# Four mixed layers on one core: weights staged further ahead, output tiles finished in pairs, elementwise work moved from GpSimd to VectorE

## The chip, the core and the metric

The kernel runs on one core of a Trainium2 chip. The core has five engines: TensorE for matrix products (PE in the profile; its weight loads are PEld), VectorE (DVE), ScalarE (ACT), GpSimd (POOL) and SyncE (SP), which here issues every DMA. The metric is the device time of one launch in microseconds. Three runs of the kernel before gave 3770.92 us in the median (3770.17 to 3778.2).

## What is computed

A sequence of 2048 tokens of width 1024, in float32, goes through four layers. Each has a wide input projection, several mixers, gates, an output projection and (but for the last) a layer norm over the residual sum. Cut to the frame, with the mixers left out:

```python
def first_block(x, w_in, lb_logits, hg_norm_w, sinks, w_out, ln_g, ln_b):   # layer 1
    h = jnp.einsum('btd,de->bte', h_res, w_in[layer])
    hq, hf, hi, hg, aq, ak, av, ag = jnp.split(h, IN_SPLITS, axis=-1)
    ...   # a gated linear recurrence (o_h) and a sliding-window attention (o_a)
    mix = jnp.concatenate([o_h, o_a], axis=-1)
    out = jnp.einsum('bte,ed->btd', mix, w_out[layer])
    z = DN_ALPHA * h_res.astype(f32) + out.astype(f32)
    mu = jnp.mean(z, axis=-1, keepdims=True)
    var = jnp.mean(jnp.square(z - mu), axis=-1, keepdims=True)
    z = (z - mu) * lax.rsqrt(var + LN_EPS)
    h_res = (z * ln_g[layer].astype(f32) + ln_b[layer].astype(f32)).astype(dt)

def reference(x, ...):
    x = first_block(x, ...)     # layer 1
    x = second_block(x, ...)    # layers 2 and 3: linear attention + spatial gating; retention + pooling
    return third_block(x, ...)  # layer 4: band attention, mLSTM, convolution; x + projection, no norm after
```

## The kernel before

**Blocks.** The tokens are cut into four blocks of 512. The blocks go in pairs: blocks 0 and 1 pass through layers 1, 2, 3 and 4 (layer 1 block 0, layer 1 block 1, layer 2 block 0, and so on), then blocks 2 and 3 do the same. So there are 16 block passes, eight per pair. Each pass loads its input (channels on the partitions, lines 521 to 549), runs the input projections, the mixers and the output projection (lines 575 to 648), and writes its result to DRAM twice: as channels (`chn`, the next layer's input) and as token rows (`rows`, the next layer's residual).

**Split numbers.** A product of float32 numbers is made of three matmuls on numbers of a shorter format: an operand is split in a high part and the rest, and high times high, high times rest and rest times high are added up in PSUM (line 324 issues each of them). For the input that is `ah` and `al`: ScalarE casts (line 548), VectorE subtracts (line 315, called by line 549).

**Weights.** A weight tile `whl` holds both parts of one piece of a weight matrix, 1 MB; there are four buffers of it. `weight` (line 439) is called for every piece. The first time that a piece is used, which is in block 0 of each layer, it is loaded unsplit into a staging tile `wst` (line 449; there are two of them), ScalarE casts it into the high half of `whl` (line 450), VectorE subtracts to get the other half (line 451, recorded as line 315), and the split pair is saved to DRAM as `wdr` (line 454). Every later use loads the split pair in one DMA, `whl<-wdr` (line 446). A `whl` buffer comes free when the last matmul that reads it is done, and only then can its next load start.

**Order of the work.** The program is written in straight Python; a scheduler in the framework places each instruction on its engine's queue by readiness and priority, and each engine then works its queue strictly in order. `weight` has a raised priority (`hp`, line 259), so weights are placed well ahead of their use. All DMAs are on SP's queue, in order too: a DMA that must wait for an engine holds up those behind it. In the first pass `load_x` keeps its DMAs in program order (lines 528 to 540): two quarter pieces of the input, a weight, two more pieces, a weight, and so on.

**The start of a pass.** Layer 1 to 4 all begin with `in_b4` (line 477): four weights give four groups of output channels, first for tokens 0 to 255 of the block (24 matmuls per group), then for tokens 256 to 511. Between the groups `flush` runs the pending pieces of the pass before (`tail`, line 650): a tail transposes one finished tile of 128 tokens on TensorE, copies it out on ScalarE, writes `chn`, applies the norm's scale and shift (lines 674 and 675, GpSimd, for tiles 0 and 2), and writes `rows`.

**The end of a pass.** The second half of the output projection (lines 609 to 643) takes four weights with two channel chunks each. It goes tile by tile: for each of the four tiles of 128 tokens all eight chunks, 24 matmuls, then on VectorE the residual sum (line 623), the norm's statistics (line 628), a chain of operations on one column (`rstd1`, line 702), and the normalisation (ScalarE for tiles 0 and 2, four VectorE operations for tiles 1 and 3). So every one of the four weights is in use until tile 3.

**GpSimd** has 408 elementwise operations with two inputs: the gates' products into `mix` (line 788 and the like), the rest parts of `split_ch` (line 570), scales and shifts, products of the rotary terms, sums of the pooling.

Of the kernel before, what the change touches and what calls it, by code (L numbers as in the profile page):

```python
# [10 lines left out]
F32 = mybir.dt.float32  # L11
# [215 lines left out]
class Build:  # L227
    def __init__(self, ctx, tc, I, O, layers=(1, 2, 3, 4), nblk=NB):
# [13 lines left out]
        self.parts = {}  # L242
# [196 lines left out]
    def weight(self, name, i, n=1024):  # L439
        nc = self.nc  # L440
        with self.hp():
            w = self.whl.tile([128, 2, n], F32R, tag="whl", name="whl")
            hi, lo = w[:, 0], w[:, 1]
            kept = self.parts.get((name, i))
# [3 lines left out]
            st = self.wst.tile([128, n], F32, tag="wst", name="wst")  # L448
            self.first(nc.sync.dma_start(st, self.I[name][i][:, 0:n]))
            nc.scalar.copy(hi, st)  # L450
            self.tt(lo, st, hi.bitcast(F32), ALU.subtract)
            if self.nblk > 1:
                kept = self.wdr.tile([128, 2, n], F32, tag=f"{name}_{i}", name="wdr")
                nc.sync.dma_start(kept, w.bitcast(F32))
                self.parts[name, i] = kept
        return hi, lo

# [63 lines left out]
    def load_x(self, b, l):  # L521
# [13 lines left out]
        self.ahead, self.start = ws, False  # L535

# [29 lines left out]
    def split_ch(self, p, k):  # L566
# [3 lines left out]
        self.tt(self.al[:, p], m, self.ah[:, p].bitcast(F32), ALU.subtract, self.nc.gpsimd)  # L570
# [4 lines left out]
    def out_proj(self, layer, b, split):  # L575
# [74 lines left out]
    def tail(self, layer, b, xr, t, lng, lnb):  # L650
# [132 lines left out]
    def gate_mix(self, accs, c0, n=512, half=None):  # L783
        for t in range(4):
# [3 lines left out]
            self.tt(m, m, g, ALU.mult, self.nc.gpsimd)  # L788
# [19 lines left out]
    def layer1(self, b, lc):  # L808
# [69 lines left out]
        for c in range(4):  # L878
# [3 lines left out]
            self.tt(m, m, g, ALU.mult, nc.gpsimd)  # L882
# [201 lines left out]
    def layer2(self, b, lc):  # L1084
# [86 lines left out]
        for t in range(4):  # L1171
# [5 lines left out]
            self.tt(s, s, sg, ALU.mult, nc.gpsimd)  # L1177
            self.tt(s, s, sb, ALU.add, nc.gpsimd)
        for t, ps in enumerate(self.in_a()):
            g = self.g()  # L1180
            self.gate(ps, g)
            self.tt(us[t], us[t], g, ALU.mult, nc.gpsimd)
# [78 lines left out]
    def layer3(self, b, lc):  # L1261
# [7 lines left out]
        for i in range(4):  # L1269
# [7 lines left out]
            self.tt(sh, sh, S, ALU.mult, nc.gpsimd)  # L1277
            self.tt(s, s, sh, ALU.add, nc.gpsimd)
# [8 lines left out]
        for g in range(4):  # L1287
# [9 lines left out]
            for l in range(g + 1):  # L1297
# [3 lines left out]
                self.tt(cur[:, start:528], prev[:, start:528], prev[:, start - d:528 - d], ALU.add, nc.gpsimd if l == 0 else None)  # L1301
# [497 lines left out]
```

## Time and profile before

| | |
|---|---|
| median of three runs | 3770.92 us (3770.17 to 3778.2) |
| the profiled execution | 3774.09 us |
| its span, first to last instruction | 3772.3 us |
| mean granted TensorE clock | 0.995 |
| TensorE busy | 3677.3 us, 20576 matmuls |
| VectorE busy | 2177.9 us, 5387 instructions |
| ScalarE busy | 1384.2 us, 2889 instructions |
| GpSimd busy | 542.1 us, 445 instructions |
| moved by DMA | 798.04 MB, 212 GB/s in the mean |

Busy times are sums over an engine's instructions; engines overlap. TensorE's busy time leaves 95 us of the span in which it has no matmul running. A row of a timeline gives the start, the duration, the engine, the line, the operation and its operands (out<-in), and in brackets how long the engine had been idle before it and what it waited for. A row with x2 or more stands for several instructions in a row, from the first one's start to the last one's end.

### The profile page before, as it was taken

The numbers are of one execution on the slowest core, as the hardware profiler recorded it, in microseconds if no ns is written. First come the engines' busy times: TensorE is split into PE (matmuls) and PEld (weight loads), VectorE is DVE, ScalarE is ACT, GpSimd is POOL, SyncE is SP. The second block draws the span as 40 slices with busy tenths as digits, with TensorE's granted clock in tenths as the row PEclk, the third lists the DMA queues.
The fourth block names the chain that finished last, engine by engine and source line by source line (L and its number), as shares of the span: only waits on it lengthen the run. The fifth ranks groups of instructions, "written<-read, shape, count | busy, mean of one in ns | idle before, by whom it ended". The sixth has DMA issues, their size and how long they took to land.

```text
span 3772.3 us, 53592 instructions
## 1 busy us (share of the span) xinstructions
PE 3677.3 (97%) x20576; PEld 3100.4 (82%) x20576; DVE 2177.9 (58%) x5387; ACT 1384.2 (37%) x2889; POOL 542.1 (14%) x445
## 2 busy tenths in 40 slices
PE   7999999999999999999999999999999999999999
PEld 6788888887888888788888878888887878888887
DVE  6765556555655598577456455443544545872873
ACT  5636343323241354325254263312221313441441
POOL 0020111112121200300200201111121311011002
PEclk9999999999999999999999999999999999999999
DMA  6775567855886576752544645747565756435434
GB/s 229 261 263 177 187 239 273 311 199 195 300 304 215 213 260 223 261 197 101 208 179 164 226 152 187 255 161 256 185 231 206 253 193 246 146 140 209 177 123 157
DMA packets 161680, 798.04 MB, mean 212 GB/s; under 512 B 17936, under 2 KB 18064, under 8 KB 93840
## 3 DMA queue, kind: packets, MB, share of 16 engines
q1 hardware_dynamic: 161424, 794.62, 58.4%
q8 instruction: 162, 2.65, 0.3%
q14 instruction: 94, 0.77, 0.1%
HBM read 593.02 MB, written 201.52 MB: 211 GB/s over the span
## 4 chain that ended last, share of the span: by engine, by line
PE 49%; DVE 6%; DMA 2%; ACT 2%; issue 1%; POOL 0%; SPq 0%; DVEq 0%; POOLq 0%; ACTq 0%
PE acc L324 41%; PE mm L324 6%; PE mm L327 3%; DVE u L312 2%; DMA whl<-wdr 1%; DVE t L315 1%; ACT t L301 0%; DVE big L312 0%; DMA wst<-in_wo_dram 0%; DVE t L1034 0%; DVE ss L1400 0%; ACT u L301 0%; POOL mix L315 0%; DVE mix L312 0%; ACT u L1424 0%
## 5 line engine op out<-in xcount | busy, mean ns | idle before, releaser
L324 PE MATMUL acc<-whl,ah 128*128 128x512 f32 (+3 forms) x6144 | 1816.2, 380 | 15.1 <-DVE whl L315 4.1
L324 PEld LDWEIGHTS acc<-whl,ah 128*128 128x128 f32 x6144 | 1112.0, 188 | 242.9 <-issue 7.1
L324 PE MATMUL acc<-whl,al 128*128 128x512 f32 (+3 forms) x3072 | 1156.8, 377 | 0.0
L324 PE MATMUL acc<-ah,whl 128*128 128x256 f32 (+1 forms) x4096 | 1076.8, 346 | 46.0 <-DVE whl L315 17.3
L324 PEld LDWEIGHTS acc<-ah,whl 128*128 128x128 f32 x4096 | 707.1, 191 | 135.0 <-DVE whl L315 18.6
L324 PE MATMUL acc<-al,whl 128*128 128x512 f32 (+1 forms) x2048 | 699.2, 342 | 0.5 <-DVE al L315 0.2
L324 PEld LDWEIGHTS acc<-whl,al 128*128 128x128 f32 x3072 | 578.0, 188 | 114.0
L324 PEld LDWEIGHTS acc<-al,whl 128*128 128x128 f32 x2048 | 391.5, 191 | 40.5 <-issue 2.9
L315 DVE TENSOR_TENSOR whl<-wst,whl 128x1024 fp32r<-128x1024 f32 (+2 forms) x140 | 173.3, 1244 | 142.0 <-ACT whl L450 131.5
L315 POOL TENSOR_TENSOR big<-big,u 128x512 f32<-128x512 f32 x96 | 139.1, 1471 | 562.0 <-PE mm L327 421.6
L450 ACT CAST whl<-wst 128x1024 fp32r<-128x1024 f32 (+2 forms) x140 | 143.3, 1027 | 149.3 <-DMA wst<-in_wi_dram 76.1
L548 ACT CAST ah<-u 128x512 fp32r<-128x512 f32 x128 | 79.3, 619 | 307.0 <-PE acc L324 200.1
L312 DVE SCALAR_TENSOR_TENSOR g<-g,acc 128x512 f32<-128x512 f32 x80 | 54.6, 686 | 204.3 <-ACT g L301 204.2
L312 DVE SCALAR_TENSOR_TENSOR u<-mix,hdw,u 128x512 f32<-128x512 f32 x240 | 165.6, 742 | 0.1
L315 POOL TENSOR_TENSOR mix<-mix,g 128x512 f32<-128x512 f32 x56 | 77.4, 1385 | 592.2 <-DVE g L312 574.2
L312 DVE SCALAR_TENSOR_TENSOR big<-big,acc 128x512 f32<-128x512 f32 x128 | 86.7, 684 | 120.2 <-PE acc L324 118.5
L301 ACT ACTIVATE g<-acc 128x512 f32<-128x512 f32 x72 | 42.6, 596 | 232.0 <-PE acc L324 226.4
L301 ACT ACTIVATE t<-mm,cols 128x128 f32<-128x128 f32 (+2 forms) x272 | 99.6, 463 | 66.6 <-PE mm L327 62.7
L315 POOL TENSOR_TENSOR u<-u,lc 128x512 f32<-128x512 f32 (+1 forms) x64 | 68.0, 1070 | 326.1 <-issue 170.0
L315 DVE TENSOR_TENSOR al<-u,ah 128x512 fp32r<-128x512 f32 x128 | 89.7, 702 | 42.1 <-ACT ah L548 41.0
L324 PE MATMUL mm<-big,u 128*128 128x256 f32 (+2 forms) x616 | 94.3, 289 | 7.3 <-ACT big L923 1.8
L324 PEld LDWEIGHTS mm<-big,u 128*128 128x128 f32 x616 | 84.3, 191 | 16.0 <-ACT u L1424 3.2
(342 smaller groups left out, 4376.8 us busy)
## 6 DMA issues: line engine op xcount, KB each, us to landing
whl<-wdr SPq DMA_DIRECT2D x396, 1024.0 KB, 4.8
wdr<-whl SPq DMA_DIRECT2D x132, 1024.0 KB, 5.3
wst<-in_wi_dram SPq DMA_DIRECT2D x100, 512.0 KB, 6.9
rows<-big SPq DMA_DIRECT2D x48, 512.0 KB, 4.0
chn<-t SPq DMA_DIRECT2D x96, 256.0 KB, 6.3
u<-chn SPq DMA_DIRECT2D x96, 256.0 KB, 6.6
big<-rows SPq DMA_DIRECT2D x48, 512.0 KB, 7.1
wst<-in_wo_dram SPq DMA_DIRECT2D x32, 512.0 KB, 6.0
```

Of the source, the lines that this page charges most:

```text
L301: return self.nc.scalar.activation(out, in_, f, bias=bias, scale=scale)
L312: return self.nc.vector.scalar_tensor_tensor(out, in0, s, in1, op0, op1)
L315: return (eng or self.nc.vector).tensor_tensor(out, a, b, op)
L324: return self.nc.tensor.matmul(out, lhsT, rhs, start=start, stop=stop)
L327: return self.nc.tensor.transpose(out, in_, self.ident)
L450: nc.scalar.copy(hi, st)
L548: nc.scalar.copy(h, c4(st))
```

## The change

Three things are done, and they are independent of each other in the code.

First, the weights. `pieces` lists every piece in the order of use. When `weight` is called for a piece that is already kept in DRAM, it now looks at the next two pieces of the list; those that are used for the first time are staged at once (`stage` issues the load into `wst`), and their own call later finds them there. In the first pass the very first weight is loaded, cast and subtracted in two column halves, the saves to `wdr` are held back (`unsaved`) and issued after the input is loaded with a lowered priority, and the layer's constants `lc` are loaded after the input and the four weights.

Second, the output projection. In its second half the tiles go in pairs: tiles 0 and 1 share one pass over the eight chunks, then tiles 2 and 3.

Third, all 408 elementwise operations of GpSimd go to VectorE. GpSimd keeps the setup, masks, fills and one small copy.

```diff
@@ -239,7 +239,7 @@
         self.bp = pool("bp", 1)
         self.dp = pool("dp", 1, space=bass.MemoryType.DRAM)
         self.wdr = pool("wdr", 1, space=bass.MemoryType.DRAM)
-        self.parts = {}
+        self.parts, self.staged, self.unsaved = {}, {}, []
         self.ps_a = pool("ps_a", 4, space=PSUM)
         self.ps_m = pool("ps_m", 4, space=PSUM)
 
@@ -441,19 +441,55 @@
         with self.hp():
             w = self.whl.tile([128, 2, n], F32R, tag="whl", name="whl")
             hi, lo = w[:, 0], w[:, 1]
+
+            assert self.order.pop(0) == (name, i, n)
+            if not self.start:
+                for a, k, m in self.order[0:2]:
+                    if (a, k) not in self.parts and (a, k) not in self.staged and (name, i) in self.parts:
+                        self.staged[a, k] = self.stage(a, k, m)
             kept = self.parts.get((name, i))
             if kept is not None:
                 nc.sync.dma_start(w.bitcast(F32), kept)
                 return hi, lo
-            st = self.wst.tile([128, n], F32, tag="wst", name="wst")
-            self.first(nc.sync.dma_start(st, self.I[name][i][:, 0:n]))
-            nc.scalar.copy(hi, st)
-            self.tt(lo, st, hi.bitcast(F32), ALU.subtract)
+            st = self.staged.pop((name, i), None) or self.stage(name, i, n)
+            parts = 2 if self.start and i == 0 else 1
+            for p in range(parts):
+                c = slice(p * n // parts, (p + 1) * n // parts)
+                nc.scalar.copy(hi[:, c], st[:, c])
+                self.tt(lo[:, c], st[:, c], hi[:, c].bitcast(F32), ALU.subtract)
             if self.nblk > 1:
                 kept = self.wdr.tile([128, 2, n], F32, tag=f"{name}_{i}", name="wdr")
-                nc.sync.dma_start(kept, w.bitcast(F32))
                 self.parts[name, i] = kept
+                self.unsaved.append((kept, w))
+                if not self.start:
+                    self.save()
         return hi, lo
+
+    def stage(self, name, i, n):
+        st = self.wst.tile([128, n], F32, tag="wst", name="wst")
+        parts = 2 if self.start and i == 0 else 1
+        for p in range(parts):
+            c = slice(p * n // parts, (p + 1) * n // parts)
+            self.first(self.nc.sync.dma_start(st[:, c], self.I[name][i][:, c]))
+        return st
+
+    def save(self):
+        while self.unsaved:
+            kept, w = self.unsaved.pop(0)
+            self.nc.sync.dma_start(kept, w.bitcast(F32))
+
+    def pieces(self):
+
+        for l, c in list(self.todo):
+            i = 0
+            for mode, cols in plan(l):
+                n = len(cols)
+                per = chunks_per_tile(n)
+                for _ in range(8 // per):
+                    yield f"wi{l}", i, per * n
+                    i += 1
+            for i in range(8):
+                yield f"wo{l}", i, 1024
 
     def next_w(self, n=1024):
         if self.ahead:
@@ -533,6 +569,9 @@
                     self.load_x1(b, l, t, i)
             ws.append(self.next_w())
         self.ahead, self.start = ws, False
+        self.lc = self.lconst(l, b)
+        with self.later(300):
+            self.save()
 
     def first(self, ins):
         if self.start:
@@ -567,7 +606,7 @@
 
         m = self.mix[:, (k - 4) * 1024 + 512:(k - 4) * 1024 + 1024]
         self.nc.scalar.copy(self.ah[:, p], m)
-        self.tt(self.al[:, p], m, self.ah[:, p].bitcast(F32), ALU.subtract, self.nc.gpsimd)
+        self.tt(self.al[:, p], m, self.ah[:, p].bitcast(F32), ALU.subtract)
 
     def mixv(self, t, k):
         return self.mix[:, t * 1024 + k * 128:t * 1024 + k * 128 + 128]
@@ -611,14 +650,13 @@
         for j in range(4):
             hi, lo = self.weight(wo, 4 + j)
             ws.append((hi.rearrange("p (k c) -> p k c", k=2), lo.rearrange("p (k c) -> p k c", k=2)))
-            if j == 0:
-                for i in range(2):
-                    for t in range(0):
-                        self.out_mm(acc[t], t, i, ws[0][0][:, i], ws[0][1][:, i])
-        for t in range(4):
-            for k in range(2 if t < 0 else 0, 8):
-                hi, lo = ws[k // 2]
-                self.out_mm(acc[t], t, k, hi[:, k % 2], lo[:, k % 2])
+        for t in range(4):
+
+            if t % 2 == 0:
+                for k in range(8):
+                    hi, lo = ws[k // 2]
+                    for t1 in (t, t + 1):
+                        self.out_mm(acc[t1], t1, k, hi[:, k % 2], lo[:, k % 2])
             x = self.xr[:, t, 512:1024]
             self.stt(x, x, alpha, acc[t], ALU.mult, ALU.add)
             if layer == 4:
@@ -671,8 +709,8 @@
         if t % 2 == 0:
             for i in range(2):
                 xi = x[:, i * 512:i * 512 + 512]
-                self.tt(xi, xi, lng[i], ALU.mult, nc.gpsimd)
-                self.tt(xi, xi, lnb[i], ALU.add, nc.gpsimd)
+                self.tt(xi, xi, lng[i], ALU.mult)
+                self.tt(xi, xi, lnb[i], ALU.add)
         nc.sync.dma_start(self.rows[layer, b % 2][t], x)
 
     def rms_row(self, b, xr):
@@ -785,7 +823,7 @@
             g = self.g((128, n)) if t < 2 else self.u((128, n))
             self.gate(accs[t][:, 0:n], g, 0.5 if half is None else half[:, t:t + 1])
             m = self.mix[:, t * 1024 + c0:t * 1024 + c0 + n]
-            self.tt(m, m, g, ALU.mult, self.nc.gpsimd)
+            self.tt(m, m, g, ALU.mult)
 
     def v_from(self, accs, scale=None):
         with self.hp():
...
@@ -1467,7 +1505,7 @@
...
-            self.tt(m, m, halves(g), ALU.mult, nc.gpsimd)
+            self.tt(m, m, halves(g), ALU.mult)
@@ -1487,8 +1525,8 @@
...
-            self.tt(x, x, cg_, ALU.mult, nc.gpsimd)
-            self.tt(x, x, cb_, ALU.add, nc.gpsimd)
+            self.tt(x, x, cg_, ALU.mult)
+            self.tt(x, x, cb_, ALU.add)
...
@@ -1750,13 +1788,14 @@
...
         self.todo = [(l, c) for b in range(0, self.nblk, 2) for l in self.layers for c in range(b, b + 2)]
         self.lc = None
+        self.order = list(self.pieces())
```

Three places show how this moves instructions. The first is SP's queue at the very start: `u` are pieces of the input, `wst` the unsplit weights, `lc` the constants, `wdr` the saved split weights. Before:

```order
L346 DMA cols_89<-in_cols_dram 128x293
L545 DMA u_193<-in_xt_dram 128x512
L545 DMA u_197<-in_xt_dram 128x512
L449 DMA wst_202<-in_wi1_dram 128x1024
L730 DMA lc_253<-in_lc1_dram 128x1280
L454 DMA wdr_206<-whl_201 128x2048
L545 DMA u_208<-in_xt_dram 128x512
L545 DMA u_212<-in_xt_dram 128x512
L449 DMA wst_217<-in_wi1_dram 128x1024
L454 DMA wdr_221<-whl_216 128x2048
L545 DMA u_223<-in_xt_dram 128x512
```

And after the change:

```order
L346 DMA cols_89<-in_cols_dram 128x293
L584 DMA u_193<-in_xt_dram 128x512
L584 DMA u_197<-in_xt_dram 128x512
L473 DMA wst_202<-in_wi1_dram 128x512 x2
L584 DMA u_210<-in_xt_dram 128x512
L584 DMA u_214<-in_xt_dram 128x512
L473 DMA wst_219<-in_wi1_dram 128x1024
L584 DMA u_224<-in_xt_dram 128x512
L584 DMA u_228<-in_xt_dram 128x512
L473 DMA wst_233<-in_wi1_dram 128x1024
L584 DMA u_238<-in_xt_dram 128x512
```

The saves and the constants no longer stand among the input's pieces, and the first weight comes in two halves.

The second is VectorE's queue where layer 1 of block 1 ends and layer 2 of block 0 begins. `acc` are output-projection sums, `big` is the residual tile, the one-column names (`vt`, `vy`, `vh`, `vf`, `mv`, `nm`) belong to the norm, `u_4378` to `u_4384` are its scales and shifts, and the `whl` that are made from `wst` are the next layer's first weights; the last two of the four that `in_b4` needs are shown. Before, at the end of tile 3:

```order
L312 SCALAR_TENSOR_TENSOR vt_4716<-vy_4715,vh_4713 128x1
L312 SCALAR_TENSOR_TENSOR vy_4715<-vt_4716,vy_4715 128x1
L312 SCALAR_TENSOR_TENSOR vt_4716<-vy_4715,vf_4714 128x1
L312 SCALAR_TENSOR_TENSOR vt_4716<-vt_4716 128x1
L312 SCALAR_TENSOR_TENSOR vy_4715<-vt_4716,vy_4715 128x1
L312 SCALAR_TENSOR_TENSOR big_3817<-big_3817,vy_4715,u_4380 128x512
L312 SCALAR_TENSOR_TENSOR big_3817<-big_3817,vy_4715,u_4381 128x512
L315 TENSOR_TENSOR whl_4872<-wst_4873,whl_4872 128x1024
L315 TENSOR_TENSOR whl_4931<-wst_4932,whl_4931 128x1024
```

After the change, from the residual sum of tile 3 (`acc_4542`); the subtraction of the third weight, `whl_4875`, stands two rows ahead of this piece, right behind tile 2's sum:

```order
L312 SCALAR_TENSOR_TENSOR big_3820<-big_3820,acc_4542 128x512
L321 TENSOR_SCALAR ve_4698<-mv_4696 128x1
L315 TENSOR_TENSOR al_97<-u_4757,ah_96 128x4x128
L321 TENSOR_SCALAR vy_4701<-ve_4698 128x1
L320 TENSOR_SCALAR vh_4699<-ve_4698 128x1
L320 TENSOR_SCALAR vf_4700<-ve_4698 128x1
L666 BN_STATS bst_4535<-big_3820 128x6
L312 SCALAR_TENSOR_TENSOR vt_4702<-vy_4701,vh_4699 128x1
L315 TENSOR_TENSOR al_97<-u_4765,ah_96 128x4x128
L312 SCALAR_TENSOR_TENSOR vy_4701<-vt_4702,vy_4701 128x1
L315 TENSOR_TENSOR big_3820<-big_3820,u_4381 128x512
L315 TENSOR_TENSOR whl_4934<-wst_4935,whl_4934 128x1024
```

The third and fourth weight stood behind tile 3's whole chain; now one stands ahead of tile 2's column chain, the other in the midst of it and ahead of tile 3's, and a scale of tile 0 (`u_4381`, an operation of GpSimd before) stands just ahead of the fourth.

The third is SP's queue at the same place: `whl<-wdr` is a kept weight, `wdr<-whl` a save, `wst` a weight to come, `chn` and `rows` the finished tiles. Before:

```order
L446 DMA whl_4546<-wdr_2292 128x2048
L676 DMA rows_123<-big_3817 128x1024
L454 DMA wdr_4769<-whl_4764 128x2048
L454 DMA wdr_4828<-whl_4823 128x2048
L449 DMA wst_4873<-in_wi2_dram 128x1024
L449 DMA wst_4932<-in_wi2_dram 128x1024
L670 DMA chn_122<-t_4800 128x512
L670 DMA chn_122<-t_4811 128x512
L676 DMA rows_123<-big_3817 128x1024
```

After the change:

```order
L452 DMA whl_4551<-wdr_2295 128x2048
L479 DMA wdr_4774<-whl_4771 128x2048
L473 DMA wst_4876<-in_wi2_dram 128x1024
L479 DMA wdr_4831<-whl_4828 128x2048
L473 DMA wst_4935<-in_wi2_dram 128x1024
L479 DMA wdr_4880<-whl_4875 128x2048
L473 DMA wst_5092<-in_wi2_dram 128x544
L708 DMA chn_122<-t_4805 128x512
L479 DMA wdr_4939<-whl_4934 128x2048
L473 DMA wst_5123<-in_wi2_dram 128x544
L708 DMA chn_122<-t_4816 128x512
L714 DMA rows_123<-big_3820 128x1024
```

The loads of the third and fourth weight stood behind two saves and behind a `rows` write; now each stands behind one save, and the `rows` write comes after the next layer's first loads.

More of the change, by code (lines that the diff above doesn't have):

```diff
@@ L881, in layer1 @@
             m = self.mix[:, c * 1024 + 512:c * 1024 + 1024]
-            self.tt(m, m, g, ALU.mult, nc.gpsimd)
+            self.tt(m, m, g, ALU.mult)
             for h in (c - 1, c, c + 1):
@@ L1176, in layer2 @@
                 self.ts(gs, gs, mv[:, 2 * i:2 * i + 1], y[:, i:i + 1], ALU.subtract, ALU.mult)
-            self.tt(s, s, sg, ALU.mult, nc.gpsimd)
-            self.tt(s, s, sb, ALU.add, nc.gpsimd)
+            self.tt(s, s, sg, ALU.mult)
+            self.tt(s, s, sb, ALU.add)
         for t, ps in enumerate(self.in_a()):
@@ L1181, in layer2 @@
             self.gate(ps, g)
-            self.tt(us[t], us[t], g, ALU.mult, nc.gpsimd)
+            self.tt(us[t], us[t], g, ALU.mult)
         for t in range(4):
@@ L1276, in layer3 @@
             self.tt(s, s, C, ALU.mult)
-            self.tt(sh, sh, S, ALU.mult, nc.gpsimd)
-            self.tt(s, s, sh, ALU.add, nc.gpsimd)
+            self.tt(sh, sh, S, ALU.mult)
+            self.tt(s, s, sh, ALU.add)
             self.tt(c4(s), c4(s), gt[:, i // 2, i % 2].unsqueeze(1).to_broadcast([128, 4, 128]), ALU.mult)
@@ L1300, in layer3 @@
                 cur = self.tb()
-                self.tt(cur[:, start:528], prev[:, start:528], prev[:, start - d:528 - d], ALU.add, nc.gpsimd if l == 0 else None)
+                self.tt(cur[:, start:528], prev[:, start:528], prev[:, start - d:528 - d], ALU.add)
                 prev = cur
@@ L1361, in layer4 @@
                 self.stt(ub[i][:, 32:544], th, 1.0, ca[i], ALU.add, ALU.mult)
-            self.tt(ub[i][:, 32:544], ub[i][:, 32:544], RS, ALU.mult, nc.gpsimd)
+            self.tt(ub[i][:, 32:544], ub[i][:, 32:544], RS, ALU.mult)
             nc.vector.tensor_copy(ub[i][:, 0:32], self.ch[:, i])
@@ L1506, in layer4 @@
             self.stt(m, ths[t], 1.0, m, ALU.add, ALU.mult)
-            self.tt(ths[t], m, m, ALU.mult, nc.gpsimd)
+            self.tt(ths[t], m, m, ALU.mult)
             nc.vector.tensor_reduce(ss[:, 4 * t:4 * t + 4].unsqueeze(2), c4(ths[t]), axis=AX.X, op=ALU.add)
@@ L1514, in layer4 @@
             m = self.mix[:, t * 1024 + 256:t * 1024 + 768]
-            self.tt(c4(m), c4(m), y[:, 4 * t:4 * t + 4].unsqueeze(2).to_broadcast([128, 4, 128]), ALU.mult, nc.gpsimd)
+            self.tt(c4(m), c4(m), y[:, 4 * t:4 * t + 4].unsqueeze(2).to_broadcast([128, 4, 128]), ALU.mult)
         def split(p):
@@ L1521, in split @@
                 nc.scalar.copy(halves(self.ah[:, p]), m)
-                self.tt(halves(self.al[:, p]), m, halves(self.ah[:, p].bitcast(F32)), ALU.subtract, nc.gpsimd)
+                self.tt(halves(self.al[:, p]), m, halves(self.ah[:, p].bitcast(F32)), ALU.subtract)
             else:
@@ L1752, in ml_head @@
         dst = self.mix.rearrange("p (t c) -> p t c", t=4)[:, :, 256 + h * 128:384 + h * 128]
-        self.tt(dst, nums[:, :, 0:128], d.unsqueeze(2).to_broadcast([128, 4, 128]), ALU.mult, nc.gpsimd)
+        self.tt(dst, nums[:, :, 0:128], d.unsqueeze(2).to_broadcast([128, 4, 128]), ALU.mult)
     def run(self):
```

## The prediction

> **What bounds the kernel now.** I began with the page's busy times and slices, then read the waits of TensorE, and then the timelines around its longest idle stretches.
>
> ```profile
> span 3772.3 us, 53592 instructions
> ...
> PE 3677.3 (97%) x20576; PEld 3100.4 (82%) x20576; DVE 2177.9 (58%) x5387; ACT 1384.2 (37%) x2889; POOL 542.1 (14%) x445
> ...
> DVE  6765556555655598577456455443544545872873
> ...
> POOL 0020111112121200300200201111121311011002
> ```
>
> TensorE is busy for 97% of the span. The change removes no matmul, so what can be won is its idle time, 3772.3 - 3677.3 = 95 us, and the stretches in which it is busy at a lower clock. The question is which of the 95 us the change reaches. The waits of TensorE (line waited for, sum in us, times, longest):
>
> ```profile
> PE acc L324 <- DVE whl L315: 21.4, 8, 6.1
> PE acc L324 <- ACT whl L450: 10.8, 3, 10.0
> PE acc L324 <- ACT ah L548: 9.7, 3, 4.3
> PE acc L324 <- DMA whl<-wdr: 7.8, 9, 2.0
> PE mm L324 <- DVE u L312: 5.8, 10, 1.2
> ...
> PE acc L324 <- DVE g L312: 2.4, 2, 2.2
> ```
>
> Four rows are waits for weights and for the first input, 49.7 us together: weights split for the first time (21.4 and 10.8), the first input (9.7), kept weights (7.8). The change touches all four. The other 45 us are many waits of about a microsecond for VectorE and ScalarE inside the mixers.
>
> **The start.** Timelines of TensorE, SP and ScalarE, and a window behind them (us, busy us and instructions of PE, PEld, DVE, ACT, POOL, then granted clock, DMA share, GB/s):
>
> ```profile
> 10.00 0.58 PE L324 MATMUL acc<-ah,whl 128*128 128x256 f32 x1 [10.00 <-ACT whl L450]
> ...
> 18.11 0.58 PE L324 MATMUL acc<-ah,whl 128*128 128x256 f32 x1 [4.35 <-ACT ah L548]
> ...
> 27.88 0.50 PE L324 MATMUL acc<-ah,whl 128*128 128x256 f32 x2 [3.46 <-ACT ah L548]
> ...
> 2.19 0.43 SPq L449 DMA_DIRECT2D wst<-in_wi_dram  x1
> ...
> 11.23 0.33 SPq L454 DMA_DIRECT2D wdr<-whl  x1
> 11.60 1.41 SPq L545 DMA_DIRECT2D u<-in_xt_dram  x2
> ...
> 8.90 1.04 ACT L450 CAST whl<-wst 128x1024 fp32r<-128x1024 f32 x1 [2.17 <-DMA wst<-in_wi_dram]
> ...
> 16.79 1.27 ACT L548 CAST ah<-u 128x512 fp32r<-128x512 f32 x2 [6.73 <-DMA u<-in_xt_dram]
> ...
> 32.00:50.00 18.00, 15.99 (x134) 15.53 (x133) 9.71 (x15) 8.25 (x14) 0.29 (x1) 1.00 0.80 287
> ```
>
> The second pair of input pieces is issued only at 11.60, because the save of the first weight stands before it on SP and waits for VectorE to finish that weight. The cast of that input comes at 16.79 and TensorE waits 4.35, later 3.46. After the change nothing that waits stands between the input's pieces, so they and the next weights follow at once. The 0.5 MB weight issued at 2.19 is there at 8.90; half a weight should come some 1.4 us earlier (half of the idle and transfer time before it) and its cast is half as long, 0.5 us less, so TensorE starts at about 8.0 instead of 10.0. At the pace of the window, 15.99 / 134 = 0.12 us, the 192 matmuls of this stretch take 23 us, plus about 4 for the slow pace that the first ones show (10.00 to 18.11). Before, they end at about 49. After: 8 + 23 + 4 = 35, a gain of 14. The upper bound, without the slow pace's full cost, is 16. The lower is 8: the four saves held back come later, 4 MB at the window's 287 GB/s are 14 us of DMA in a stretch that already uses 0.80 of it, and part of that may show as a wait for the next weights. I take **-14**.
>
> **The three changes of layer in the first pair of blocks.** TensorE, SP, GpSimd, VectorE and ScalarE where layer 1 goes over to layer 2, and the same wait at another change:
>
> ```profile
> 521.39 0.80 PE L324 MATMUL acc<-ah,whl 128*128 128x256 f32 x2 [5.57 <-DVE whl L315]
> ...
> 1307.07 0.80 PE L324 MATMUL acc<-ah,whl 128*128 128x256 f32 x2 [6.07 <-DVE whl L315]
> ...
> 522.00:527.00 5.00, 5.00 (x26) 5.00 (x26) 0.47 (x1) 0.00 (x0) 0.00 (x0) 0.53 1.04 392
> ...
> 503.28 1.66 SPq L454 DMA_DIRECT2D wdr<-whl  x2
> 504.99 2.29 SPq L449 DMA_DIRECT2D wst<-in_wi_dram  x2
> ...
> 508.14 10.85 POOL L315 TENSOR_TENSOR big<-big,u 128x512 f32<-128x512 f32 x8 [47.18 <-DVE nm L312]
> ...
> 505.36 0.68 DVE L312 SCALAR_TENSOR_TENSOR big<-big,acc 128x512 f32<-128x512 f32 x1
> 505.95 0.21 DVE L312 SCALAR_TENSOR_TENSOR vt<-vy,vh 128x1 f32<-128x1 f32 x1
> ...
> 511.60 1.24 DVE L312 SCALAR_TENSOR_TENSOR vt<-vy,vh 128x1 f32<-128x1 f32 x1
> ...
> 520.12 2.35 DVE L315 TENSOR_TENSOR whl<-wst,whl 128x1024 fp32r<-128x1024 f32 x2
> ...
> 508.40 1.24 ACT L301 ACTIVATE big<-big,nm,vy 128x1024 f32<-128x1024 f32 x1
> ```
>
> Two of the four weights that begin the new layer are late: VectorE makes them only at 520.12, behind the whole norm of tile 3. And that norm is slow: a one-column operation that took 0.21 at 505.95 takes 1.24 at 511.60, in the stretch from 508.14 in which GpSimd runs eight operations. The wait is 5.57 here and 6.07 at the third change; with the rest of the row of 21.4, three changes cost about 17. Behind each, the clock falls to half: 26 matmuls in 5.00 us is 0.19 each, and 26 x (0.19 - 0.12) = 1.9 us are lost; with the few before the window about 2.2. Together 17 + 3 x 2.2 = 23.5. Three edits act here: tiles in pairs release the first weight's buffer after about 14 of the 22.4 us of this half instead of 18 (of 96 matmuls the last that reads it is number 60 instead of 78, at 0.23 us each); SP's queue has one save instead of two before the third and fourth `wst`; and nothing runs on GpSimd. By the order, the third and fourth subtraction stand ahead of tile 3's norm. So the wait should go.
>
> What is late next is tile 2, which now ends with tile 3 and whose transposes stand on TensorE behind 79 matmuls and 16 transposes of the new layer, some 11 us after the projection's end. On VectorE, from its residual sum to `nm`, stand 12 rows of 512 columns at 0.59 (505.36 to 505.95), two weights at 1.2 and 11 small ones at 0.2: 11.7 us, of which 0.7 lie before the projection's end, and then 1.24 on ScalarE: ready at 12.2. A new wait of about 1.3 at each change, 4 in all. I take 23.5 - 4, so **-19**; bounds -23.5 and -12 (if those new waits lower the clock again and some weight stays late).
>
> **Kept weights at the other ends of a pass.**
>
> ```profile
> 1905.23 0.36 PE L324 MATMUL acc<-ah,whl 128*128 128x256 f32 x1 [2.00 <-DMA whl<-wdr]
> ...
> 1906.00:1909.00 3.00, 3.00 (x16) 3.00 (x15) 0.00 (x0) 0.00 (x0) 0.00 (x0) 0.50 1.02 431
> ...
> 1888.34 10.37 SPq L625 DMA_DIRECT2D out_dram<-big  x3
> 1899.06 4.52 SPq L446 DMA_DIRECT2D whl<-wdr  x4
> ```
>
> Four loads are issued from 1899.06 on, behind output writes that wait for each tile's sum; TensorE waits 2.00, and 16 matmuls in 3.00 us at granted clock 0.50 lose another 16 x 0.07, with those beside it 1.7. With pairs the buffers come free earlier, and only tiles 0 and 1 stand ahead of the loads; in the other layers the loads now stand ahead of the `rows` writes. All of 7.8 + 1.7 would be -9.5; I take **-8**, with -4 as the bound if loads at the DMA's limit (share 1.02) stay late.
>
> **GpSimd's work on VectorE.** Groups of both engines (busy, mean ns):
>
> ```profile
> L315 POOL TENSOR_TENSOR big<-big,u 128x512 f32<-128x512 f32 x96 | 139.1, 1471 | 562.0 <-PE mm L327 421.6 <-DVE nm L312 93.5 <-DVE bst L628 45.5
> ...
> L315 DVE TENSOR_TENSOR t<-t,lc 128x512 f32<-128x512 f32 x40 | 25.9, 688 | 0.5
> ```
>
> 408 operations at no more than 0.69 us add 281 us to VectorE's 2177.9: at most 2459, 65% of the span. Each takes half of its time on GpSimd, so a chain through it gets shorter when VectorE is free, and longer by what stands in its queue when not. The cover is TensorE's own work; if it is gone, the price is rival D. The waits of this kind (5.8 and 2.4 of the rows above) may go or grow: I take **-2**, bounds -8 and +6.
>
> In the Trainium skill, the page "SBUF — State Buffer", section "SBUF: two separate sides", says that a VectorE operation with two SBUF inputs and a GpSimd operation that reads SBUF share a port pair as an exclusive lock, and that the loser waits out the other's whole instruction. The trace agrees: 1.24 us for one column is close to one of GpSimd's eight, 10.85 / 8 = 1.36. By that rule every such collision ends, which is rival C's side.
>
> **The end of the kernel.** Tiles 2 and 3 end together, so one sum of 0.68 and part of one output write come later: **+1**.
>
> The sum is -14 - 19 - 8 - 2 + 1 = -42. The profiled execution took 3774.1 (span 3772.3), which is 3.2 above the median; it becomes 3732, and the median 3770.9 - 42 = **3729**.
>
> **Rivals.**
>
> *B: tile 2 is late.* The new wait at the changes of layer is longer than worked out, and lowers the clock each time: 3 x (1.3 + 2.2) = 10.5 instead of 4, and the same at some ends within a layer, another 4: -42 + 10.5 = -31, so 3740. For it: VectorE has more to do at exactly this point. Against: the wait is short beside the 5.57 that went before. In the Trainium skill, "TensorE: Matmul & The Clock Gate", section "Part 1: The HAM clock gate (the "warmup" mystery)", the clock falls after at least one idle window of some 3.4 us; here the wait of 2.00 already brought 0.50, so the trace doesn't bear out a limit that high. By the page B would be 3 x 1.3 alone, which is my forecast.
>
> *C: more goes than the weights' waits.* Every term comes at its good end, -16 - 23.5 - 9.5 - 8 + 1 = -56: 3715. For it: VectorE's operations that ran beside GpSimd get shorter (1.24 to 0.21). Against: most of them had TensorE's work as cover.
>
> *D: VectorE becomes the bound in layer 4 (slower).* There VectorE's slices read 9 and 8.
>
> ```profile
> 3150.00:3400.00 250.00, 245.17 (x1462) 210.22 (x1461) 192.46 (x469) 110.27 (x234) 32.32 (x29) 1.00 0.48 173
> ...
> 1500.00:1550.00 50.00, 46.18 (x227) 36.77 (x227) 37.74 (x88) 18.95 (x37) 24.67 (x22) 1.00 0.41 152
> ```
>
> A pass of layer 4 (250 us) has 29 operations on GpSimd, 20 us on VectorE. If all of them lay on the path that ends the pass, four passes would cost 80: -42 + 80 = +38, so 3809; it is slower from 10.5 us per pass on. Against it: VectorE is idle for 250 - 192 = 57.5 us in that pass, the slices with 9 or 8 have a 0 for GpSimd, and where GpSimd is busiest, from 1500 on, VectorE has 12 us left and loses its own collisions.
>
> *E: the order of the weights changes nothing.* The late weights wait for the DMA and not for buffers, and only the start is won: 3757. For it: the first two were staged ahead already. Against: the rows show the third and fourth held by SP's and VectorE's queues.
>
> **How the numbers follow.** Forecast 0.58, B 0.18, C 0.11, D 0.07, E 0.06. A measurement here can tell 0.2%, 7.5 us, from no change. Forecast, B, C and half of E are faster by more than that: 0.90; the other half of E, with the start's gain at its bound of 8, is no change: 0.03; D is slower: 0.07. The range takes in C and B with their margins, and leaves out D and most of E: 3704 to 3750.
>
> **What would show it.** In the profile after: TensorE's first matmul at about 8.0, and no wait over 2 us before 36; no row of 5 us for `whl` at the changes of layer, but waits of 1 to 2 us for a transpose's input some 11 us behind the projection; the `whl<-wdr` row under 4 us; VectorE at 2300 to 2460 us busy and one-column operations at 0.2 throughout; TensorE's idle time near 55 us. It is wrong if that idle time stays over 75, if waits for VectorE inside the mixers pass 60 us, or if half-clock stretches still follow each change of layer.

## The result and the profile after

The changed kernel takes 3688.95 us in the median (3688.44 to 3690.86), against 3773.11 for the kernel before in the same group of runs: a ratio of 0.9776, with a 95% interval of 0.976 to 0.9793. That is 84 us less, twice the 42 that were forecast, and 15 below the end of the range. The sign was right, the size was not.

The page of the changed kernel:

```profile
span 3687.4 us, 53350 instructions
...
PE 3651.2 (99%) x20576; PEld 3089.5 (84%) x20576; DVE 2252.7 (61%) x5796; ACT 1386.2 (38%) x2890; POOL 14.7 (0%) x37
```

TensorE's time without a matmul falls from 95 us to 3687.4 - 3651.2 = 36. Its busy time falls too, by 26 us for the same 20576 matmuls, in part because it runs less often at the lower clock: its matmuls ran for 34 us at half clock before and run for 10 now, which is 12 of the 26 (the mean granted clock goes from 0.995 to 0.998). What the other 14 are is not shown. VectorE got 409 instructions more and is busy only 2252.7 - 2177.9 = 75 us longer. That row is the surprise: 408 operations at up to 0.69 us should have added up to as much as 281. About 200 us must have come off the operations that VectorE had before.

The waits of TensorE in the changed kernel (line waited for, sum in us, times, longest):

```profile
PE acc L324 <- ACT whl L458: 7.0, 1, 7.0
PE mm L327 <- DVE big L312: 5.5, 3, 2.2
PE mm L327 <- DVE nq L312: 4.3, 4, 1.1
PE mm L324 <- DVE u L312: 3.7, 8, 0.6
...
PE mm L327 <- ACT big L301: 1.0, 2, 0.6
...
PE acc L324 <- DVE whl L315: 0.5, 1, 0.5
...
PE acc L324 <- ACT ah L587: 0.2, 1, 0.2
```

Of the four rows that stood for 49.7 us before, the waits for weights and for the first input, the very first wait, 7.0, is left, and rows of 0.5 and 0.2. The row for kept weights (`whl<-wdr`, 7.8) is gone altogether. The places that the prediction spoke of, in the changed kernel: TensorE's first matmul, the stretch of the start, the tile whose transposes might be late where layer 1 goes over to layer 2, and a one-column operation of VectorE there:

```profile
6.98 0.58 PE L324 MATMUL acc<-ah,whl 128*128 128x256 f32 x1 [6.98 <-ACT whl L458]
...
0.00:34.00 34.00, 25.98 (x198) 24.98 (x199) 22.36 (x62) 17.36 (x28) 3.10 (x14) 1.00 0.89 324
...
498.33 1.09 PE L327 MATMUL mm<-ident,big 128*128 128x128 f32 x8 [0.59 <-ACT big L301]
...
498.73 0.22 DVE L312 SCALAR_TENSOR_TENSOR vt<-vy,vh 128x1 f32<-128x1 f32 x1
```

TensorE starts at 6.98 and has done 198 matmuls by 34 us. Before, it had done as many by 50, as the window of the kernel before says:

```profile
0.00:50.00 50.00, 29.35 (x198) 27.61 (x199) 21.88 (x60) 16.68 (x26) 3.09 (x14) 0.97 0.66 229
```

The wait of 5.57 for `whl` has become one of 0.59 for tile 2. And the one-column operation, which took 1.24 at this place, takes 0.22.

Where the 84 us lie, from the first matmul of each of the 16 passes to the first of the next (read off TensorE's timelines of the two profiled executions, in us):

| pass | before | after | difference |
|---|---|---|---|
| layer 1, block 0 (with the start) | 266.5 | 246.8 | -19.7 |
| layer 2, block 0 | 216.8 | 207.3 | -9.5 |
| layer 3, block 0 | 189.2 | 179.1 | -10.1 |
| layer 4, block 0 | 311.6 | 288.8 | -22.8 |
| layers 1 to 4, block 1 | 921.1 | 920.8 | -0.3 |
| layers 1 to 4, blocks 2 and 3 | 1867.1 | 1844.6 | -22.5 |

In block 1, layer 4 gains 5 and the other layers lose 1.3 to 1.7 each, which is no loss: where a layer goes on to its next block, the transposes of tiles 0 and 1 (16 in 1.9 us) stood ahead of the first matmul before and stand behind it now, so the pass before is shorter by as much. Finer than by passes, the starts of the same matmul can be set side by side in the two timelines: both have 20576, in the same order but for the ends of the passes. The beginning of a pass is taken here from 120 matmuls before its first to 260 after. So read, in one profiled execution of each kernel, 16 us are won at the start, 25 at the three changes of layer (7.9, 7.9 and 9.5), 17 where the other twelve passes begin, and 27 inside the passes, 12 of them in layer 4 of block 0. On the last two the forecast had put little.

### The profile page after: what moved, and what is told of

Read it like the earlier page. It is cut to its first block, busy times and chain, and to the rows that moved or that the text cites. A ratio compares the mean times of both kernels' runs of the same rounds, so it can differ in the third digit from the quotient of the medians.

```text
span 3687.4 us, 53350 instructions
## 1 busy us (share of the span) xinstructions
PE 3651.2 (99%) x20576; PEld 3089.5 (84%) x20576; DVE 2252.7 (61%) x5796; ACT 1386.2 (38%) x2890; POOL 14.7 (0%) x37
## 4 chain that ended last, share of the span: by engine, by line
PE 58%; DVE 5%; ACT 2%; issue 0%; DMA 0%; POOL 0%; SPq 0%; POOLq 0%; DVEq 0%; ACTq 0%
PE acc L324 48%; PE mm L324 7%; PE mm L327 3%; DVE u L312 1%; DVE t L315 1%; ACT t L301 0%; DVE big L312 0%; DVE t L1072 0%; ACT u L301 0%; ACT t L302 0%; DVE ss L1438 0%; DVE t L312 0%; DVE whl L315 0%; ACT big L301 0%; ACT u L1462 0%
## 5 line engine op out<-in xcount | busy, mean ns | idle before, releaser
L324 PE MATMUL acc<-ah,whl 128*128 128x256 f32 (+1 forms) x4096 | 1064.4, 344 | 7.7 <-ACT whl L458 7.0
L324 PEld LDWEIGHTS acc<-ah,whl 128*128 128x128 f32 x4096 | 698.1, 188 | 90.6 <-ACT whl L458 7.0
L324 PEld LDWEIGHTS acc<-al,whl 128*128 128x128 f32 x2048 | 386.2, 189 | 41.2 <-issue 3.9
L315 DVE TENSOR_TENSOR whl<-wst,whl 128x1024 fp32r<-128x1024 f32 (+3 forms) x141 | 167.1, 1186 | 106.1 <-ACT whl L458 103.4
L458 ACT CAST whl<-wst 128x1024 fp32r<-128x1024 f32 (+3 forms) x141 | 143.4, 1019 | 168.6 <-PE acc L324 114.1
L1021 DVE CUSTOM_DVE_ANT_0 t<-mm,lc,nsk 128x256 f32<-128x256 f32 (+1 forms) x128 | 55.0, 472 | 51.0 <-PE mm L324 50.7
L324 PEld LDWEIGHTS mm<-vb,t 128*128 128x128 f32 (+1 forms) x640 | 67.8, 169 | 15.3 <-issue 9.8
L324 PE MATMUL mm<-vb,t 128*64 128x128 f32 (+2 forms) x640 | 79.1, 278 | 1.0 <-DVE tb L1674 1.0
```

The source lines that it names most:

```text
L315: return (eng or self.nc.vector).tensor_tensor(out, a, b, op)
L324: return self.nc.tensor.matmul(out, lhsT, rhs, start=start, stop=stop)
L458: nc.scalar.copy(hi[:, c], st[:, c])
L1021: nc.vector.tensor_tensor_reduce(out=p[:, o + off:o + 256], in0=ps[:, o + off:o + 256], in1=band[:, off:256], scale=-0.125, scalar=self.ns ...
```

## The experiments

All medians are in us. Each group of four kernels ran on one chip with its own runs of the kernel before (3773.92, 3771.72 and 3773.01 in the median).

### Each part alone, and two without the third

**GpSimd's work moved, nothing else.** In the kernel before, all 408 operations go to VectorE, as here:

```diff
-            self.tt(m, m, g, ALU.mult, self.nc.gpsimd)
+            self.tt(m, m, g, ALU.mult)
```

> The kernel before with its 408 elementwise operations moved from GpSimd to VectorE, and nothing else changed. Theory 1 (the three parts act on separate waits and add up): the third and fourth weight still stand behind tile 3's norm on VectorE and the start is untouched, so about 20 us of the 84 come from the small waits inside the passes and perhaps 10 at the changes of layer because the norm runs faster: 3735 to 3750. Theory 2 (what held VectorE back at every place was GpSimd running beside it): most of the gain is here, 3710 to 3725, and the 5 us waits for whl at the changes of layer are gone or under 2 us. If the operations cost as much as they free, it stays at 3770.

Measured: 3723.85, ratio 0.9869 (0.9854 to 0.9884), 50 us less. This is in theory 2's range, near its upper end, and outside what theory 1 allowed. The row of TensorE for `whl` from VectorE falls from 21.4 to 3.8, its longest wait to 2.0.

**Tiles in pairs, nothing else.**

```diff
-        for t in range(4):
-            for k in range(2 if t < 0 else 0, 8):
-                hi, lo = ws[k // 2]
-                self.out_mm(acc[t], t, k, hi[:, k % 2], lo[:, k % 2])
+        for t in range(4):
+            if t % 2 == 0:
+                for k in range(8):
+                    hi, lo = ws[k // 2]
+                    for t1 in (t, t + 1):
+                        self.out_mm(acc[t1], t1, k, hi[:, k % 2], lo[:, k % 2])
```

> The kernel before with the second half of the output projection two tiles at a time, and nothing else changed. Theory 1: the four waits at the changes of layer and the kept weights go, about -25 to -35, so 3738 to 3748, and the row of whl<-wdr falls under 2 us. Theory 2: the subtractions are still slowed by GpSimd, and only the kept weights come earlier: -8 to -12, so about 3760.

Measured: 3748.26, ratio 0.9936 (0.9921 to 0.9951), 26 us less: 0.3 above theory 1's range. But theory 1's other mark failed: the row for `whl<-wdr` is 5.9, where under 2 was expected.

**The weights' part, nothing else** (the changed start, the look-ahead, the held saves).

> The kernel before with the changed start and the weights staged ahead, tiles one at a time and GpSimd as before. Both theories: TensorE begins at 7 instead of 10 us and the first pass is 16 us shorter; staging ahead moves little by itself, since the first two weights of a layer were staged already: 3753 to 3758. If staging ahead matters, the changes of layer get shorter too: under 3745.

Measured: 3758.4, ratio 0.9964 (0.9949 to 0.9978), 15.5 us less, 0.4 above the range. TensorE begins at 8.13 and the first pass is 14 us shorter, where 7 and 16 were expected.

**Weights and pairs, GpSimd's work left on GpSimd.**

> The changed kernel with the 408 operations back on GpSimd: pairs and weights alone. Theory 1: start and weights' waits are won, the small waits inside the passes and half-clock stretches stay: about -50, 3720 to 3730. Theory 2: VectorE is slowed at each end of a pass, the waits for whl come back in part: -20 to -30, 3740 to 3750.

Measured: 3732.52, ratio 0.9895 (0.9881 to 0.991), 41 us less, 2.5 above theory 1's range. Of its page and of TensorE's waits:

```profile
span 3729.9 us, 53637 instructions
...
PE 3660.1 (98%) x20576; PEld 3088.7 (83%) x20576; DVE 2206.2 (59%) x5388; ACT 1384.4 (37%) x2890; POOL 538.4 (14%) x445
...
PE mm L327 <- ACT t L301: 6.2, 9, 0.7
PE mm L324 <- DVE u L312: 5.3, 10, 1.2
PE mm L327 <- ACT big L301: 5.1, 3, 2.2
```

TensorE is without a matmul for 3729.9 - 3660.1 = 69.8 us here, against 36.2 when GpSimd's work is moved too.

Read together: 15.5 and 25.7 add up to 41.2, and both together measure 41.4, so nothing shows that these two touch each other. Moving GpSimd's work is worth 50 on the kernel before, and 3732.5 - 3689 = 43.6 on top of the other two. The 6.5 us between are hardly more than the interval of one of these ratios (5 to 6 us to either side).

Place by place, though, pairs and GpSimd's work do touch. With the same matmul set side by side as above, GpSimd's work alone wins 24 us at the three changes of layer, pairs alone 18, and all three parts together 25: there each wins most of what the other would. Where the other twelve passes begin it is the other way round: 5 and 0 alone, 17 together. How it comes about at a change, the timelines of TensorE show where layer 1 goes over to layer 2, with the weights' part alone, GpSimd's work alone, and pairs alone:

```profile
507.31 0.79 PE L324 MATMUL acc<-ah,whl 128*128 128x256 f32 x2 [5.57 <-DVE whl L315]
```

```profile
511.95 0.39 PE L324 MATMUL acc<-ah,whl 128*128 128x256 f32 x1 [0.21 <-ACT whl L450]
```

```profile
516.71 1.09 PE L327 MATMUL mm<-ident,big 128*128 128x128 f32 x8 [2.21 <-ACT big L301]
```

The changed staging leaves the wait of 5.57 as it was. Moving GpSimd's work takes it away although the third and fourth subtraction still stand behind tile 3's norm in VectorE's queue: the norm alone is now quick enough. Pairs take it away by the order, and get the new wait for tile 2 in its place, 2.21 with GpSimd still at work and 0.59 without. So neither theory holds at the change of layer as stated; both causes were there, and taking away one was enough for most of the gain.

**The look-ahead taken out of the changed kernel** (the changed start stays).

```diff
-            if not self.start:
-                for a, k, m in self.order[0:2]:
-                    if (a, k) not in self.parts and (a, k) not in self.staged and (name, i) in self.parts:
-                        self.staged[a, k] = self.stage(a, k, m)
```

> The changed kernel without the staging two pieces ahead (the changed start stays). Prediction: the first two weights of a new layer were loaded early before too, so it costs 0 to 4 us: 3689 to 3693. If staging ahead carried the changes of layer, waits for whl come back there, 3 x 5: 3700 to 3706.

Measured: 3689.6, 0.7 us above the changed kernel's first median: no difference. As far as these runs can tell, all that the weights' part wins is the start.

### What GpSimd costs VectorE

**The 96 scales and shifts at the ends of the passes back on GpSimd**, in the changed kernel.

```diff
-                self.tt(xi, xi, lng[i], ALU.mult)
-                self.tt(xi, xi, lnb[i], ALU.add)
+                self.tt(xi, xi, lng[i], ALU.mult, nc.gpsimd)
+                self.tt(xi, xi, lnb[i], ALU.add, nc.gpsimd)
```

> The changed kernel (3688.95) with only the 96 scales and shifts at the ends of the passes back on GpSimd. Theory 2 (GpSimd running beside VectorE holds it back): the VectorE operations beside them stretch again and the ends of the 12 passes that have them get longer, +8 to +20: 3697 to 3709. Theory 3 (the move helps because VectorE does each operation in half the time and so shortens the chain that waits for it): nobody on TensorE waits for these 96 operations, they end in a DMA of rows, so within 4 us of 3689, or faster, since VectorE has less to do.

Measured: 3709.91, ratio to the kernel before 0.984 (0.9825 to 0.9855), so 21 us slower than the changed kernel and 0.9 above theory 2's range, though VectorE has 96 operations less and no matmul waits for these results. Side by side, 9 us are lost at the changes of layer and 12 where the other passes begin, none inside the passes.

**The other 312 back on GpSimd**, the scales and shifts left on VectorE.

> The changed kernel with the 312 operations of the mixers and gates back on GpSimd and the 96 scales and shifts left on VectorE. If the 44 us that lie between pairs and weights alone (3732.5) and the changed kernel (3689) are made up of collisions place by place, this is the other part of what the scales and shifts cost (21): +20 to +25, 3708 to 3715. If only the ends of the passes matter, within 5 us of 3689.

Measured: 3716.54, ratio 0.9852 (0.9838 to 0.9867). The changed kernel in the same group gave 3690.08, so this part is worth 26.5, a little over what was expected; 21 and 26.5 make 47 where the two together were 43.6. Here 24 us are lost inside the passes.

> The changed kernel unaltered, as the measure for the others of this group: 3687 to 3691.

Measured: 3690.08, ratio 0.9781 (0.9767 to 0.9796).

These two runs still move work to and fro. The next two don't.

**Useless work on GpSimd.** In the changed kernel, with nothing moved, GpSimd gets 96 multiplications whose results nobody reads, started by `nm` of tiles 0 and 2 through a copy of one column; the second kernel has fills in their place.

```diff
+                nc.vector.tensor_copy(self.jos[t // 2][:, 0:1], nm)
+                for i in range(4):
+                    self.tt(self.jos[t // 2], self.jk, self.jos[t // 2], ALU.mult, nc.gpsimd)
                 self.act(x, x, AF.Identity, scale=y, bias=nm)
```

```diff
+                nc.vector.tensor_copy(self.jos[t // 2][:, 0:1], nm)
+                for i in range(10):
+                    nc.gpsimd.memset(self.jos[t // 2], 0.0)
                 self.act(x, x, AF.Identity, scale=y, bias=nm)
```

> The changed kernel with 96 additional multiplications on GpSimd at the same places, on scratch tiles that nobody uses (each group of four starts when nm of tile 0 or 2 is there; the results are thrown away). No work of the kernel moves. Theory 2: VectorE's operations beside them stretch to 1.2 us and more, and the time rises as with the scales and shifts on GpSimd or a little more: 3697 to 3712. Theory 3: nothing waits for them, so within 3 us of 3689.

> The same as the kernel with additional multiplications, but GpSimd fills the scratch tiles ten times instead of multiplying four times: about the same busy time, and it reads nothing. If what collides is reading by GpSimd, VectorE keeps its durations and the time is within 3 us of 3689; if any work of GpSimd collides, it is like the multiplications, 3697 to 3712.

Measured: 3728.29 with the multiplications, ratio to the kernel before 0.989 (0.9874 to 0.9907), 39 us slower than the changed kernel and beyond the expected range. 3690.71 with the fills, ratio 0.9786 (0.9771 to 0.98): no difference. The busy times and groups of the two, first with the multiplications:

```profile
PE 3664.5 (98%) x20576; PEld 3099.0 (83%) x20576; DVE 2346.4 (63%) x5823; ACT 1384.9 (37%) x2890; POOL 170.3 (5%) x133
...
L312 DVE SCALAR_TENSOR_TENSOR vt<-vy,vh 128x1 f32<-128x1 f32 x48 | 35.0, 730 | 0.0
...
L315 POOL TENSOR_TENSOR jo<-jk,jo 128x512 f32<-128x512 f32 x96 | 156.2, 1627 | 1893.4 <-DVE jo L679 1217.0 <-DVE ve L321 670.7
```

And with the fills:

```profile
PE 3653.4 (99%) x20576; PEld 3091.8 (84%) x20576; DVE 2254.1 (61%) x5823; ACT 1385.3 (38%) x2890; POOL 140.6 (4%) x277
...
L312 DVE SCALAR_TENSOR_TENSOR vt<-vy,vh 128x1 f32<-128x1 f32 x48 | 10.2, 214 | 0.0
...
L681 POOL MEMSET jo<- 128x512 f32 x240 | 126.4, 527 | 1884.9 <-DVE jo L679 1208.3 <-DVE ve L321 664.1
```

And the waits of TensorE for the tiles that the norm finishes, a row of 1.0 in the changed kernel, with the multiplications:

```profile
PE mm L327 <- ACT big L301: 15.6, 11, 3.6
```

VectorE has the same 5823 instructions in both. Beside 156 us of useless multiplications it is busy 2346.4, beside 126 us of useless fills 2254.1, as in the changed kernel without either (2252.7). So 94 us of VectorE's time, and 39 us of the kernel's, come from nothing but GpSimd multiplying at the same time. That is theory 2 with nothing else in play, and theory 3, the shorter chain, doesn't explain it. Nor is it enough that GpSimd is at work at the same moment: 24 of the 48 one-column operations shown (`vt`) ran while GpSimd was multiplying and took 1245 ns in the mean; 24 ran while it was filling and took 212.

The multiplications cost more than the 21 us of the scales and shifts, and the same operations show a likely reason: the multiplications start with `nm`, in the midst of the norm of the other tiles, and slow 24 of the 48; the scales and shifts on GpSimd slow 2. Of the 39 us, 20 are lost at the changes of layer and 18 where the other passes begin.

The same groups in the kernel before and in the changed one show whose operations stretch. Before:

```profile
L312 DVE SCALAR_TENSOR_TENSOR big<-big,mv,u 128x512 f32<-128x512 f32 x48 | 56.5, 1177 | 0.0
...
L312 DVE SCALAR_TENSOR_TENSOR g<-g,acc 128x512 f32<-128x512 f32 x80 | 54.6, 686 | 204.3 <-ACT g L301 204.2
...
L321 DVE TENSOR_SCALAR u<-u,mv,y 128x128 f32<-128x128 f32 x64 | 36.6, 633 | 0.1
...
L312 DVE SCALAR_TENSOR_TENSOR vt<-vy,vh 128x1 f32<-128x1 f32 x48 | 21.7, 453 | 0.0
```

After:

```profile
L312 DVE SCALAR_TENSOR_TENSOR g<-g,acc 128x512 f32<-128x512 f32 x80 | 54.9, 687 | 173.0 <-ACT g L301 172.7
...
L312 DVE SCALAR_TENSOR_TENSOR big<-big,mv,u 128x512 f32<-128x512 f32 x48 | 35.7, 743 | 0.0
...
L321 DVE TENSOR_SCALAR u<-u,mv,y 128x128 f32<-128x128 f32 x64 | 20.0, 342 | 0.1
...
L312 DVE SCALAR_TENSOR_TENSOR vt<-vy,vh 128x1 f32<-128x1 f32 x48 | 10.3, 215 | 0.0
```

Operations that take all their operands from SBUF have a mean of 1177, 633 and 453 ns before and 743, 342 and 215 after. Those with an operand from PSUM (`acc`) keep theirs, 686 and 687. These means mix two kinds. Before, 37 of the 48 one-column operations met no work of GpSimd and took 218 ns, and 11 met it and took 1244. The two bigger kinds go from 743 up to 1729 and from 339 up to 1450. So one that is held back takes up to about a microsecond longer, whatever its size. Of the 80 operations with an operand from PSUM, 28 ran beside GpSimd's work, and took 686 like the others.

### Two attempts to go further

In the changed kernel TensorE's longest wait behind the start is for `big`, three times in layer 4, where the band attention's queries and keys stand on VectorE between the operations of a convolution. The first kernel gives their evictions (lines 1457 to 1466) a raised priority:

```diff
+                    with self.hp():
                     if g < 2:
                         x, xl = qh[2 * g + i], ql[2 * g + i]
...
```

> The changed kernel with the evictions of the band attention's queries and keys in layer 4 placed with raised priority, ahead of the convolution's operations that stand between them on VectorE. The three waits of TensorE for big there (5.5 us together) should go, and with them the half clock behind each: -3 to -8, 3681 to 3686. If the convolution then ends later and is waited for, no gain.

Measured: 3690.64, ratio 0.9783 (0.9766 to 0.9799), where the changed kernel beside it gave 3690.08: no gain. The wait was not taken away. The row, which the changed kernel has as 5.5, 3, 2.2:

```profile
PE mm L327 <- DVE big L312: 6.6, 4, 1.8
```

The second kernel also writes the output of layer 4 in two halves:

```diff
+            else:
+                nc.sync.dma_start(self.O[b * TB + t * 128:b * TB + t * 128 + 128, 0:512], x)
...
-                nc.sync.dma_start(self.O[b * TB + t * 128:b * TB + t * 128 + 128, :], self.xr[:, t])
+                nc.sync.dma_start(self.O[b * TB + t * 128:b * TB + t * 128 + 128, 512:1024], x)
```

> The same, and layer 4 writes the first 512 columns of each output tile when they are ready instead of whole tiles at the end. The last write is half as long, so the 6 us behind the last matmul shrink by about 1: -1 to -2 against the kernel with raised priority alone. The price could be that the writes delay the weights' loads on SP's queue.

Measured: 3688.91, ratio 0.9777 (0.9761 to 0.9794), 1.7 below the kernel with raised priority, which these runs cannot tell from nothing. Neither beats the changed kernel.

## Why the prediction was right and wrong

**The start: right.** Forecast -14, with TensorE starting at 8.0; the weights' part alone measured -15.5, nearly all of it here, and TensorE starts at 6.98. The held saves cost nothing that shows in TensorE's waits.

**Changes of layer, kept weights, the end: right in the sum, in part by luck.** The forecast had -19 - 8 + 1 = -26 for these; pairs alone measured -25.7, and start and pairs together, forecast at -40, measured -41.4. Place by place it comes out otherwise. In the changed kernel the three changes give 25 and not 19, more than the bound of 23.5. Pairs alone give 18 there, 4 at the wait of 2.00 for a kept weight that the prediction shows, -4 at the other beginnings of a pass, and 8 inside passes, which no term of the forecast names. The prediction also let three edits act together at the change of layer and gave no price to each. The runs do: staging ahead is worth nothing, pairs remove most of the wait by the order, and quick norms remove it without pairs.

**Tile 2's new wait: smaller.** Forecast 1.3 us at each change, from a queue of 11.7 us on VectorE. It was 0.59 at the first, and the row shown has 1.0 for two waits. It is 2.21 when GpSimd still works beside it. Rival B, in which this wait grows and lowers the clock, did not come: in the changed kernel's profile the clock is at half only from 48, 1352 and 1635 us on, for 3.4 us each, and at the very end, and none of these is a change of layer.

**GpSimd's work on VectorE: the step that failed.** The prediction put -2 here, with bounds of -8 and +6, and the runs put -43.6 (-50 without the other two edits). The mechanism was named in the text: 0.21 against 1.24, with the sentence that every such collision ends. What was wrong is the size of the term. The sum took 281 us of additional work for VectorE as the thing to be hidden, and counted the relief only where TensorE's wait rows named VectorE, 5.8 and 2.4 us. It should have counted the relief on VectorE itself: one group of 128x512 stood at 1177 ns where others with as many elements stood at 686 and 688, and the one-column group at 453 where single ones took 0.21 us. About 200 of the 281 us came back that way (281 - 75 = 206). And the price could not be read off the rows that name VectorE: the collisions sat at the ends of the passes (21 us) and in the mixers (26.5), where a late VectorE shows as short waits of TensorE for others too, such as the nine for ScalarE's `t`, 6.2 us, which are gone in the changed kernel. Of the 43.6 us, 69.8 - 36.2 = 34 are time of TensorE without a matmul. The lower clock has no part in them: it is granted at 0.999 with pairs and weights alone and at 0.998 in the changed kernel. By place, some 8 of the 43.6 lie at the changes of layer, which the prediction had under another term, 15 where other passes begin and 20 inside the passes. Rival C had this direction, and its 3715 failed by the same bound of -8.

**Rival D, VectorE as the bound in layer 4:** it did not come. Layer 4 of block 0 got 22.8 us shorter, not longer, and its other three passes 4 to 5 us each. The argument against it, 57.5 us of idle time in such a pass, was right and too weak, since VectorE's own work shrank as well. **Rival E:** half of it was so. Staging ahead did nothing, as it said; the gain at the changes of layer came from pairs and from GpSimd's work.

**The marks that were named:** no wait over 2 us before 36 and no 5 us row for `whl`, as said; VectorE at 2253 lies below the 2300 to 2460 named; TensorE's idle time is 36 and not near 55. Both misses point at the same term. The new waits for a transpose's input are 0.6 and less, below the 1 to 2 named.

## What to carry to other kernels

Where GpSimd multiplies or adds tiles in SBUF while VectorE works on SBUF too, the price of an operation on GpSimd is not its own duration alone but what it adds to VectorE's: compare the mean of a VectorE group with that of a group of equal size that has an operand from PSUM, or with its fastest instances. Here 408 moved operations cost VectorE 75 us instead of 281. And price every edit by itself: two of the edits here each removed most of the same wait, and a third that was meant for it did nothing.

## What the runs showed of the hardware

What GpSimd does matters, not that it works. 96 multiplications that read two tiles cost 39 us and lengthened VectorE's busy time by 94; 240 fills with a similar busy time (126 us against 156) cost nothing that can be measured and changed VectorE's busy time by 1.4. In the Trainium skill, the page "SBUF — State Buffer", section "SBUF: two separate sides", calls the port pair that VectorE and GpSimd share an exclusive lock, which a VectorE operation with two SBUF inputs takes only against a GpSimd operation that reads SBUF. The trace agrees with both halves of that: beside fills the one-column operations keep their 212 ns, and beside GpSimd's work the groups with an operand from PSUM keep theirs, 686 and 687. The slowed group of 128x128 (`u<-u,mv,y`) reads one tile and two columns; which of its operands holds it back, no run here separates.

GpSimd's operations are slowed in turn. In the kernel before, 23 of the 96 scales and shifts ran while VectorE had nothing to do and took 1291 ns in the mean; the other 73 took 1528. The useless multiplications, none of which found VectorE at rest, took 1627.
